# Interleave of two tensors on one core: the first store waits for the second output buffer

## The chip, the core and the metric

The kernel runs on one core of one Trainium2 chip. The time is device microseconds of one execution on that core. The kernel before has a median of 314.26 us over three runs (314.20 to 314.34).

## The reference

Two float32 tensors `x` and `y` of shape 32 x 256 x 1024 are interleaved along the last axis. Nothing is added or multiplied; every input element is copied once to its new place.

```python
result = np.zeros((batch, seq, dim * 2), dtype=np.float32)
result[..., 0::2] = x
result[..., 1::2] = y
```

Each input is 33.55 MB and the output is 67.11 MB, so at least 134.22 MB cross between HBM and SBUF.

## The kernel before, in words

**Tiles.** Each input is seen as one flat list and cut into n = 8 chunks of 128 partitions x 8192 floats (W = 8192), 4.19 MB each. A partition's row of a chunk is 32 KB and contiguous in HBM. A chunk k of `x` and a chunk k of `y` make 8.39 MB of output, which is woven and stored in two halves h = 0 and h = 1 of 4.19 MB. In what follows x2 or y2 is chunk 2 of an input, and store (1,0) is half 0 of chunk 1 of the output.

**Buffers.** There are two buffers for each input (`xt`, `yt`, chosen by the parity of k) and two output buffers (`ot`, chosen by h: half 0 always goes through `ot[0]`, half 1 through `ot[1]`).

**Loads (L45 to L55)** are issued on SyncE's queue (SP; queue q1 of the profile). Only the second half of x0 is issued on ScalarE's queue (L46). The first chunks, x0, y0, x1 and y1, are issued at the start, since there are buffers for them. From chunk 2 on, L50 makes the load of x_k wait until half 1 of chunk k-2 has had its `x` taken out of the buffer, and L54 makes the load of y_k wait for the same with `y`.

**Weaving (L57 to L70)** is done by VectorE (DVE). For every half, L67 copies 4096 columns of `xt` into the even columns of an output buffer, and L70 copies 4096 columns of `yt` into the odd ones. Each copy raises the semaphore `woven` by one, so that a half is ready at every second count: (0,0) at 2, (0,1) at 4, (1,0) at 6. Before L67 writes an output buffer again, L66 waits until the store that last read this buffer has landed.

**Stores (L72 to L78)** are issued on ScalarE's queue (ACT; queue q10 of the profile), in the order (0,0), (0,1), (1,0), (1,1) and so on. Before each one L74 waits for the `woven` count that its half needs. Each half is one DMA of 4.19 MB, except (0,0), which `parts` cuts in two: a first one of 128 x 2048 floats (1.05 MB, called piece a below) and a second one of 128 x 6144 floats (3.15 MB, piece b). ScalarE does no other work in the meantime; its queue is a list of waits and DMA issues, taken in order.

**What sets the order.** Nothing is planned by a scheduler here: the three lists (loads on SP, copies on DVE, stores on ACT) run in the written order, each held only by its semaphore waits. The two first loads are moved ahead of the opening barrier by `tile_interleave_kernel`; the change does not touch that.

**The end (L80 to L86).** ScalarE waits for all stores of half 0, SyncE for all of half 1, and the semaphores are cleared.

Of the kernel before, what the change touches and what calls it, by code (L numbers as in the profile page):

```python
# [3 lines left out]


def _interleave(nc, x, y, out):
    P = 128
    W = 8192
    H = W // 2  # L10

    total = 1
    for s in x.shape:
        total *= s
    n = total // (P * W)
    assert n * P * W == total

    def rows(ap, names, k):
        flat = ap.rearrange("b s d -> (b s d)")
        return flat[k * names : (k + 1) * names].rearrange("(p w) -> p w", p=P)  # L20

    fp32 = mybir.dt.float32
    xt = [nc.alloc_sbuf_tensor(f"xt{b}", [P, W], fp32).ap() for b in (0, 1)]
    yt = [nc.alloc_sbuf_tensor(f"yt{b}", [P, W], fp32).ap() for b in (0, 1)]
    ot = [nc.alloc_sbuf_tensor(f"ot{b}", [P, W], fp32).ap() for b in (0, 1)]

    xsem = [nc.alloc_semaphore(f"xsem{b}") for b in (0, 1)]
    hsem = nc.alloc_semaphore("hsem")
    ysem = [nc.alloc_semaphore(f"ysem{b}") for b in (0, 1)]
    woven = nc.alloc_semaphore("woven")  # L30
    osem = [nc.alloc_semaphore(f"osem{b}") for b in (0, 1)]

    xs = [rows(x, P * W, k) for k in range(n)]
    ys = [rows(y, P * W, k) for k in range(n)]
    os_ = [rows(out, 2 * P * W, k) for k in range(n)]

    Q = W // 4

    def parts(k, h):
        return [slice(0, W)] if k or h else [slice(0, Q), slice(Q, W)]  # L40

    def stored(k, h):
        return 16 * sum(len(parts(j, h)) for j in range(k))

    nc.sync.dma_start(out=xt[0][:, :H], in_=xs[0][:, :H]).then_inc(xsem[0], 16)  # L45
    nc.scalar.dma_start(out=xt[0][:, H:], in_=xs[0][:, H:]).then_inc(hsem, 16)  # L46
    for k in range(n):
        b = k % 2
        if k >= 2:
            nc.sync.wait_ge(woven, 4 * (k - 2) + 3)  # L50
        if k:
            nc.sync.dma_start(out=xt[b], in_=xs[k]).then_inc(xsem[b], 16)
        if k >= 2:
            nc.sync.wait_ge(woven, 4 * (k - 2) + 4)  # L54
        nc.sync.dma_start(out=yt[b], in_=ys[k]).then_inc(ysem[b], 16)  # L55

    for k in range(n):  # L57
        b = k % 2
        for h in (0, 1):
            c = slice(h * H, (h + 1) * H)  # L60
            if h == 0:
                nc.vector.wait_ge(xsem[b], 16 * (k // 2 + 1))
            elif k == 0:
                nc.vector.wait_ge(hsem, 16)
            if k:
                nc.vector.wait_ge(osem[h], stored(k, h))  # L66
            nc.vector.tensor_copy(out=ot[h][:, 0::2], in_=xt[b][:, c]).then_inc(woven, 1)  # L67
            if h == 0:
                nc.vector.wait_ge(ysem[b], 16 * (k // 2 + 1))
            nc.vector.tensor_copy(out=ot[h][:, 1::2], in_=yt[b][:, c]).then_inc(woven, 1)  # L70

    for k in range(n):  # L72
        for h in (0, 1):
            nc.scalar.wait_ge(woven, 4 * k + 2 * h + 2)  # L74
            for c in parts(k, h):
                nc.scalar.dma_start(
                    out=os_[k][:, h * W : (h + 1) * W][:, c], in_=ot[h][:, c]
                ).then_inc(osem[h], 16)  # L78

    nc.scalar.wait_ge(osem[0], stored(n, 0))  # L80
    used = sorted(s.num for s in [*xsem, hsem, *ysem, woven, osem[0]])
    assert used == list(range(used[0], used[-1] + 1)), used
    nc.scalar.sem_clear(range(used[0], used[-1] + 1))
    nc.sync.nop(nofuse=True).wait_op(osem[1], stored(n, 1), "sem-ge").then_inc(
        osem[1], -stored(n, 1)
    )  # L86


def kernel(tc, x, y, out):
    nc = tc.nc  # L90
    tc.close()
    tc.compile()

    _interleave(nc, x, y, out)

    blocks = nc.main_func.blocks
    for engine in (mybir.EngineType.SP, mybir.EngineType.Activation):
        opening = blocks[0].instructions
        at, moved = next(
            (b, i)  # L100
            for b in blocks[1:]
            for i in b.instructions
            if i.engine == engine and i.opcode == "DMACopy"
        )
        assert not (moved.sync_info and moved.sync_info.on_wait)
        body = at.instructions
        body.remove(moved)
        gate = next(
            n
            for n, i in enumerate(opening)  # L110
            if i.engine == engine and i.opcode == "Drain"
        )
        opening.insert(gate, moved)
        at.instructions = body
        blocks[0].instructions = opening


# [1 line left out]
_INS = ['x', 'y']  # L119
_OUTS = [((32, 256, 2048), 'float32')]  # L120


# [23 lines left out]
```

## Time and profile before

| what | value |
|---|---|
| median of three runs | 314.26 us |
| the profiled execution: its time | 314.21 us |
| the profiled execution: its span | 312.9 us |
| bytes moved | 134.22 MB (67.11 read, 67.11 written) |
| mean DMA rate over the span | 429 GB/s |
| share of 16 DMA engines: q10 (stores) and q1 (loads) | 51.3% and 48.5% |
| DVE busy | 71.9 us (23%), 32 copies of about 2.29 us |
| one 4.19 MB store, from issue to landing, median | 34.1 us |

The span goes from the first to the last instruction; the time of the execution is 1.3 us longer. The DMA shares are those of all 16 engines that move the data; both queues run on the same 16. A row of 128 partitions is split evenly, so each 4.19 MB transfer is 128 packets of 32 KB, eight on each engine. A DMA issue on a queue takes about 0.34 us of the issuing engine and says nothing of when the data moves: "to landing" does.

### The profile page before, as it was taken

The page shows a single profiled execution, that of the slowest core. Times are in us where ns is not written, and L with a number is a line of the kernel's source. Part 1 is how long each engine was busy: PE and PEld are TensorE (multiplying, and loading weights), DVE is VectorE, ACT ScalarE, POOL GpSimd, SP SyncE. Part 2 cuts the span into 40 slices and gives each one's busy share as a digit, 9 for nine tenths or more (in the row PEclk, how much of TensorE's full clock was granted, in tenths as well). Part 3 has the DMA queues.
Part 4 walks back from the last instruction along what each step waited for, and adds up shares of the span by engine and source line. Part 5 has one row for each costly group of instructions (what it writes and reads, how often), then busy time and mean ns, then how long its engine had stood idle before and what let it go on. Part 6 is the DMA issues. An engine that isn't in the chain of part 4 may idle for free.

```text
span 312.9 us, 114 instructions
## 1 busy us (share of the span) xinstructions
DVE 71.9 (23%) x32; POOL 0.2 (0%) x4
## 2 busy tenths in 40 slices
DVE  0216000501305023050230503205032050415400
POOL 0000000000000000000000000000000000000000
DMA  8999999999999999999999999999999999999998
GB/s 344 461 406 431 436 402 431 440 465 406 448 423 431 440 406 465 402 469 402 469 402 465 406 457 415 436 436 419 452 402 469 402 469 402 469 402 461 411 444 360
DMA packets 4896, 134.22 MB, mean 429 GB/s; under 512 B 544, under 2 KB 544, under 8 KB 544
## 3 DMA queue, kind: packets, MB, share of 16 engines
q10 hardware_dynamic: 2592, 69.21, 51.3%
q1 hardware_dynamic: 2304, 65.01, 48.5%
HBM read 67.11 MB, written 67.11 MB: 429 GB/s over the span
## 4 chain that ended last, share of the span: by engine, by line
DMA 82%; DVE 12%; issue 0%
DMA out_dram<-ot 76%; DMA yt<-in_y_dram 7%; DVE ot L70 6%; DVE ot L67 6%
## 5 line engine op out<-in xcount | busy, mean ns | idle before, releaser
L67 DVE COPY ot<-xt 128x4096 f32<-128x4096 f32 x16 | 36.7, 2295 | 218.0 <-DMA out_dram<-ot 206.3
L70 DVE COPY ot<-yt 128x4096 f32<-128x4096 f32 x16 | 36.6, 2288 | 8.0 <-DMA yt<-in_y_dram 8.0
L130 POOL MEMSET const-uint8-127<- 128x1 uint8 x1 | 0.1, 102 | 0.0
L130 POOL MEMSET const-bfloat16-1.0<- 128x1 bf16 x1 | 0.1, 101 | 0.0
L130 POOL MEMSET const-float32-0.0<- 128x1 f32 x1 | 0.1, 98 | 0.2 <-issue 0.2
L130 POOL MEMSET const-float32-1.0<- 128x1 f32 x1 | 0.1, 98 | 0.0
## 6 DMA issues: line engine op xcount, KB each, us to landing
out_dram<-ot ACTq DMA_DIRECT2D x15, 4096.0 KB, 34.1
yt<-in_y_dram SPq DMA_DIRECT2D x8, 4096.0 KB, 41.5
xt<-in_x_dram SPq DMA_DIRECT2D x7, 4096.0 KB, 24.4
out_dram<-ot ACTq DMA_DIRECT2D x1, 3072.0 KB, 32.8
xt<-in_x_dram SPq DMA_DIRECT2D x1, 2048.0 KB, 11.7
xt<-in_x_dram ACTq DMA_DIRECT2D x1, 2048.0 KB, 13.4
out_dram<-ot ACTq DMA_DIRECT2D x1, 1024.0 KB, 16.1
```

What stands on the lines that cost most here:

```text
L67: nc.vector.tensor_copy(out=ot[h][:, 0::2], in_=xt[b][:, c]).then_inc(woven, 1)
L70: nc.vector.tensor_copy(out=ot[h][:, 1::2], in_=yt[b][:, c]).then_inc(woven, 1)
L130: nc = _bacc.Bacc("TRN2", target_bir_lowering=False, num_devices=1)
```

## The change

The wait ahead of the first store asks for `woven` = 4 in place of 2. All other waits keep their values. The store of (0,0), in its two pieces, is therefore issued when (0,1) is woven as well, and the wait of (0,1), also 4, is then met already.

```diff
     for k in range(n):
         for h in (0, 1):
-            nc.scalar.wait_ge(woven, 4 * k + 2 * h + 2)
+            nc.scalar.wait_ge(woven, 4 * k + 2 * (h if k else 1) + 2)
             for c in parts(k, h):
                 nc.scalar.dma_start(
                     out=os_[k][:, h * W : (h + 1) * W][:, c], in_=ot[h][:, c]
                 ).then_inc(osem[h], 16)
```

No instruction is added, removed or moved on any engine; the lists of all five stand as before.

## The prediction

> **What bounds the kernel now.** I read the chain that ended last first, because it says whose work sets the end. In order of time (start us, us, what), its beginning is:
>
> ```profile
> 1.57 20.43 DMA yt<-in_y_dram
> ...
> 22.02 2.29 DVE ot L70
> 24.32 2.20 DVE ot L67
> 26.52 2.21 DVE ot L70
> ...
> 28.75 48.06 DMA out_dram<-ot
> ...
> 76.84 2.29 DVE ot L67
> 79.14 2.21 DVE ot L70
> ...
> 81.37 34.17 DMA out_dram<-ot
> ```
>
> The reader is to see that the chain runs through the weave of both halves of chunk 0, then through store (0,1), and from there alternates between a store and the 4.5 us weave behind it. Taken alone, this would say that every store sits on the path. But a store of 4.19 MB takes 34 to 48 us here, so it is not alone on the engines. Next I therefore read how fast the DMA engines move bytes, in four stretches (us, DVE, POOL, clock, DMA share, GB/s):
>
> ```profile
> 12.00:24.00 12.00, 3.98 (x2) 0.00 (x0) 1.00 1.00 431
> 24.00:46.00 22.00, 4.72 (x3) 0.00 (x0) 1.00 0.99 414
> 46.00:276.00 230.00, 53.96 (x24) 0.00 (x0) 1.00 1.00 434
> 277.00:312.00 35.00, 8.99 (x4) 0.00 (x0) 1.00 1.01 434
> ```
>
> From 12 to 24 only loads run, since no store has been issued (the first issue is at 24.35). From 46 to 276 loads and stores alternate. From 277 on only stores run: the last load is issued at 236.3, and its last packet ends at 276.2 in the trace's packet records. All three move 431 to 434 GB/s with all 16 engines busy (a window counts whole packets, so 431 and 434 are one rate). **The bound is bytes through 16 busy engines**, whichever way the bytes go: 134.22 MB / 434 GB/s = 309.3 us of the 312.9 us span. The rest is 1.0 us until the first packet, some 0.7 us of slow first packets, 0.4 us behind the last packet, and a loss in the stretch from 24 to 46, treated below.
>
> The third view is who waited for whom (total us, times, longest):
>
> ```profile
> DVE ot L67 <- DMA out_dram<-ot: 206.3, 14, 28.9
> DVE ot L67 <- DMA xt<-in_x_dram: 11.7, 1, 11.7
> DVE ot L70 <- DMA yt<-in_y_dram: 8.0, 1, 8.0
> ```
>
> DVE waits for loads only at the very start; after that, only for stores to free an output buffer. Its idle time costs nothing as long as the engines always hold some packet.
>
> **The change part by part.** *The wait.* The half (0,0) is woven at 24.31 (22.02 + 2.29), and piece a is issued at 24.35. The fourth copy ends at 28.72 (26.43 + 2.29), and store (0,1) is issued at 28.75. So pieces a and b go from 24.35 to 28.75, **4.4 us later**. Behind them on ACT stands only (0,1): it follows two issues of 0.34 to 0.46 us, so it is issued at about 29.6 in place of 28.75. That costs nothing, for it stands behind a and b in the same queue, and before the change b landed only at 57.5 (about 24.7 + 32.8). DVE's four copies and the loads of x2 (26.55) and y2 (28.75) hang on `woven` counts that this wait does not touch, and stay. SP and POOL are passed by nothing.
>
> *What runs in the 4.4 us.* x1 and y1, issued at 1.95 and 2.48, are 8.39 MB, 19.3 us at 434 GB/s, and start behind y0 at about 21. x2 and y2 join by 28.75. So the load queue has work to 40 by itself and, with x2 and y2, to about 60. The packet records show the first store packet only at 28.5, 4.1 us behind the issue; it should now be at about 32.9. Until then the engines carry loads at the 431 GB/s of the first row: **no byte of engine time is lost**, 0 us. If that cover were missing, the price would be the whole 4.4 us.
>
> *What is moved.* While both queues hold work, they share the engines packet by packet: (0,1) took from 57.5 to 76.84, 19.3 us for 4.19 MB, or 217 GB/s, half of 434. So stores run 4.4 us later, and loads 4.4 us earlier (0.95 MB at 217 GB/s each). Store (0,1) landed at 76.84; now that is at most 81.2. y2 landed at 84.15 (28.75 + 55.4, the longest landing of its line); now that is 79.8, its last packet near 78.2 (1.6 us earlier, as before). Here a stall goes in and must be priced. x3 can be issued only when the first copy of (1,1) ends, 2.3 us behind the landing of (0,1). Before, that was 79.16, 3.4 us before the load queue ran out at 82.6. Now **the load queue runs dry first**: at 78.2, with x3 issued at 82.8 to 83.5 (stores speed up a little once alone) and its first packet up to 4.1 us later. That is 5 to 9 us without loads.
>
> *Who covers that.* Store (1,0), issued near 66.5, holds 4.19 MB, 9.7 us at the 434 GB/s of the last row. It has the engines from about 79.3 to 89. Store (1,1) must be issued by then: (0,1) lands at about 80.8 (1.5 us behind its last packet), and 4.5 us of weaving give 85.3, 3.7 us ahead. So the engines stay busy, 0 us. Stores move ahead by just what loads lose; the lead that the loads had over the copies shrinks from some 34 us (y2 landed at 84.15, used at 117.86) to a few us, and the load queue should not run dry again before its end.
>
> *The end.* There the stores run alone in both kernels, and the last rows above are unchanged: (7,0) and (7,1) are issued 4.5 us behind the landing of the store two before. All bytes still pass at one rate, so what the first store lost is given back when the load queue is empty. Sum: **0 us**.
>
> *The unknown.* From 24 to 46 the profile lost (434 - 414) / 434 x 22 = 1.0 us; window edges are in that figure, and in the packet records about 0.5 us of it is real: between 27 and 32.2 the load packets of x1 took up to 1.59 us in place of 1.21, while the first stores came in. What slows them no view tells. If the first store joins after x1 is done, this can go (-0.5, at most -1.0), stay, or come a second time when x3 joins the stores (+0.5, at most +1.0). I take 0 as the middle, nearest to the row that shows it once.
>
> The sum is made against the profiled execution, 314.21 us, 0.05 below the median of 314.26: **314.2 us**.
>
> A rule speaks against the change. The Trainium skill, "DMA: Bandwidth & Descriptors", section "Rules for kernel authors", asks to issue a DMA early and wait for it late, so that its fixed cost lies beside other work; taken as a rule for time, it makes a store that is issued 4.4 us later dear, where the row of 12 to 24 says that the engines are full without it. It is the first rival.
>
> **The rivals.** *The delay stays (slower).* If the store chain simply moves, 314.2 + 4.4 = 318.6 us. It speaks for this that stores are 76% of the chain. It decides from the point where stores, once alone, would not run above the 217 GB/s that they have beside loads; the last row, 434 alone, speaks against it. Chance 0.05.
>
> *The stores run out in the dry stretch (slower).* If a store issued behind another also needs the 4.1 us that the first one needed, (1,1) would move at 89.4 against an end of (1,0) at 89: 0.4 us of idle engines. Were the stretch to return for each of the seven chunks left, that is 2.8 us, 317.0. Against it: from 277 to 312 the same handover happens twice without a dent. Chance 0.06.
>
> *The slow packets go (faster).* 313.2 to 313.7 us, as bounded above. Chance 0.10, of which 0.06 lies beyond 0.2%. *They come twice.* 314.7 to 315.2. Chance 0.05, of which 0.03 lies beyond 0.2%.
>
> *The change does not take effect* cannot be: the wait asks for 4, and (0,1) waited for the same 4 until 28.75.
>
> **How the numbers follow.** The forecast has 0.74. A measurement of this kernel can tell some 0.2%, 0.63 us, from no change. Faster: 0.06. Slower: 0.05 + 0.06 + 0.03 = 0.14. Same: the rest, 0.80. The range from 313.5 to 315.2 holds the forecast, most of the case in which slow packets go and all of that in which they come twice; the first rival and the dear end of the second stay outside.
>
> **What would show it.** In the profile after: piece a, b and (0,1) issued one behind the other from 28.75; the second chunk's first copy near 62 (57.60 before); (0,1) landed at 80 to 81.2; x3 issued at 82 to 83.5; its landing longer or shorter by the queue it meets; loads later at the end (past 276.2, near 280); windows of 434 GB/s throughout, and the last copy within 1 us of 295.7. Wrong would be: a window of 10 us behind 46 that is well below 434, an end that moves with the 4.4 us, or copies that wait for loads behind 30 us.

## The result and the profile after

The changed kernel took 317.73 us in the median of 13 executions, against 314.28 us for the kernel before in 13 executions of the same session. The ratio of the two, taken over the executions, is 1.0068, 95% interval 1.0043 to 1.0093; it is below the 1.011 of the two medians because the times of the changed kernel fall in groups. (A ratio leaves out executions over 1.5% above the fastest of their kernel: here two, 319.49 and 319.98, and in e17 below three of six, 329.38 to 334.13.) The forecast was 314.2 us, no change. What the median hides is the spread: the 13 times of the kernel before lie between 314.19 and 314.68, those of the changed kernel in groups, four at 314.4 to 314.7, one at 316.1, and the rest at 317.6 to 320.0. The kernel can run as forecast, and mostly does not.

The profiled execution took 318.31 us with a span of 317.0 us. The chain that ended last begins as the forecast said (start us, us, what):

```profile
26.46 2.21 DVE ot L70
...
28.70 0.36 ACTq L76
...
29.09 33.23 DMA out_dram<-ot
...
62.42 2.30 DVE ot L67
64.72 2.20 DVE ot L70
66.92 14.57 another core or an unknown queue
...
81.51 2.30 DVE ot L67
...
275.99 21.62 DMA out_dram<-ot
...
297.64 2.29 DVE ot L67
```

Piece a is issued at 28.70, the first copy of (1,0) starts at 62.42 (about 62 was forecast), that of (1,1) at 81.51 (80 to 81.2, so 0.3 us beyond). The piece of 14.57 us is the wait for store (0,1), for which this view finds no releaser. The last line is where the loss shows: the last weave starts at 297.64, and it was 293.51 before.

The rate of the DMA engines, in the same stretches as before with one added behind (us, DVE, POOL, clock, DMA share, GB/s):

```profile
12.00:24.00 12.00, 3.98 (x2) 0.00 (x0) 1.00 1.01 437
24.00:46.00 22.00, 4.67 (x3) 0.00 (x0) 1.00 0.99 417
46.00:276.00 230.00, 53.97 (x24) 0.00 (x0) 1.00 1.00 431
277.00:312.00 35.00, 8.99 (x4) 0.00 (x0) 1.00 1.01 433
312.00:317.00 5.00, 0.00 (x0) 0.00 (x0) 1.00 0.17 72
```

The reader is to see two things. The stretch from 24 to 46 lost no more than before (417 against 414 GB/s), and the long one fell from 434 to 431, which is 1.6 us of 230. And there is a tail: from 312 to 317 the engines are 17% busy. In a finer cut of the same view the rate falls most from 80 to 100. First the kernel before, then the changed one:

```profile
80.00:100.00 20.00, 5.02 (x3) 0.00 (x0) 1.00 0.99 428
```

```profile
80.00:100.00 20.00, 8.61 (x4) 0.00 (x0) 1.00 1.00 416
```

The share stays at 1.00 while the rate falls: the engines are not idle, their packets take longer. This is the stretch in which the load queue runs dry and joins again:

```profile
81.51 2.30 DVE L67 COPY ot<-xt 128x4096 f32<-128x4096 f32 x1 [14.60 <-DMA out_dram<-ot]
83.72 2.29 DVE L70 COPY ot<-yt 128x4096 f32<-128x4096 f32 x1
83.84 0.33 SPq L52 DMA_DIRECT2D xt<-in_x_dram  x1
86.04 0.33 SPq L55 DMA_DIRECT2D yt<-in_y_dram  x1
86.04 0.36 ACTq L76 DMA_DIRECT2D out_dram<-ot  x1
```

In the timeline from 80 to 100, x3 is issued at 83.84 and store (1,1) at 86.04. By the packet records the last load packet before ends at 79.75 and the next starts at 88.24, a dry stretch of 8.5 us (5 to 9 were forecast). Store (1,0) fills it, as forecast; no engine stands idle for more than 0.2 us. The waits are those of before as well, with no copy waiting for a load behind 30 us:

```profile
DVE ot L67 <- DMA out_dram<-ot: 210.5, 14, 33.8
DVE ot L67 <- DMA xt<-in_x_dram: 11.6, 1, 11.6
DVE ot L70 <- DMA yt<-in_y_dram: 8.0, 1, 8.0
```

So nearly every event came as forecast, and yet 4 us are lost. What no table of means shows is in the packet records. Each of the 16 engines ends its share of a transfer with a completion of its own, so the 16 completions of a transfer tell how far apart the engines are (first completion in us, and the time to the last of the 16):

```
                     before             after
y1                   46.2  +0.33        42.7  +0.75
y2                   83.4  +0.33        78.5  +2.42
store (1,0)          95.5  +0.33        91.9  +3.64
x4                  141.5  +0.33       145.6  +4.06
store (7,1), last   312.2  +0.33       312.9  +3.74
```

Before, the 16 engines stay within 0.33 us of each other from 46 us to the end. After, four of them fall behind: in the last store 12 engines are done within 0.2 us of 312.9, the other four 2.7, 2.8, 3.0 and 3.7 us later. So of the 4.1 us that the last completion comes later, 0.7 are on all engines and 3.4 are the lag of the last. The time goes to packets that take longer than the 1.21 us of a 32 KB packet, up to 2.42: behind 50 us the extra time sums to 1.20 us for each engine in the mean, 0.94 of it from 70 to 101 (0.78 from 80 to 100), against none before, and most of it falls on a few engines. The records do not name an engine, but an engine's next packet starts where its last one ended, so its packets can be strung together. Strung so, the four engines with the slow packets are four that took their first store packet at 32.2 to 32.4, one turn (one load packet) ahead of the twelve others (33.2 to 33.7): from 50 to 101 us they lost 2.4 us each in the mean, the others 0.45. **The rate of 16 engines is a mean; the end is that of the slowest one.**

The Trainium skill, "DMA: Bandwidth & Descriptors", section "Why a DMA increments its semaphore by 16 and not by 1", says that each engine posts its own increment behind its data and that only the full 16 means landed. The trace agrees: store (1,0) was complete on 12 engines at 92.2, and the copy that waited for it started at 95.89, when the last of the 16 had come at 95.5.

### The profile page after: what moved, and what is told of

The parts are those of the page before. It is cut to its first block, busy times and chain, and to the rows that moved or that the text cites. A ratio compares the mean times of both kernels' runs of the same rounds, so it can differ in the third digit from the quotient of the medians.

```text
span 317.0 us, 114 instructions
## 1 busy us (share of the span) xinstructions
DVE 72.0 (23%) x32; POOL 0.2 (0%) x4
## 4 chain that ended last, share of the span: by engine, by line
DMA 76%; DVE 13%; another core or an unknown queue 5%; issue 0%; ACTq 0%; DVEq 0%
DMA out_dram<-ot 70%; DVE ot L70 7%; DVE ot L67 6%; DMA yt<-in_y_dram 6%; ACTq L76 0%; DVEq L66 0%
## 5 line engine op out<-in xcount | busy, mean ns | idle before, releaser
L67 DVE COPY ot<-xt 128x4096 f32<-128x4096 f32 x16 | 36.7, 2295 | 222.2 <-DMA out_dram<-ot 210.5
## 6 DMA issues: line engine op xcount, KB each, us to landing
out_dram<-ot ACTq DMA_DIRECT2D x1, 3072.0 KB, 33.2
```

## The experiments

The theory after the result is **lag**: a few engines get slow packets and fall behind, and the end waits for them. Its forms differ in what starts it: R, the second joining of the loads after the dry stretch; J, the late first store as such; B, transfers of the two queues that end nearly together; P, engines that take the two queues in another order than the rest. Times are medians with the range of all executions, beside 314.2 to 314.3 for the kernel before in the same session.

**e1_after_again.** The changed kernel once more, no edit.

> The changed kernel once more, to see its spread. Theory (lag): when one DMA queue joins the other, a few of the 16 engines fall out of step and lose some us, and the end waits for the slowest of them; the time then varies by execution between about 314.4 and 320, and in the profile the 16 completions of the last store are spread by as much as the time stands above 314.4 (0.3 us spread at 314.4, 3.7 us at 318.3). Rival (delay): the 4.4 us of the first store stay in part and the spread of completions is chance; then time and spread do not go together.

Measured: 318.21 us (315.54 to 320.38, 6 executions), ratio 1.0111 (1.0084 to 1.0139). The profiled execution, 317.74 us, had its last completions at 312.7 +3.28: 13 engines on time and three late by 2.8 to 3.3 us. The three are again those that took their first store packet a turn ahead of the rest (32.2 to 32.5 against 33.2 to 33.6). Time above 314.4 and spread are near each other, 3.3 and 3.28 here, 3.9 and 3.74 in the first profile; in slower runs they are not, for e3 and e17 below end with 3.73 at 325.38 and 322.48 us. There store (6,0) has to land on the slowest engine too before (7,0) can be woven into its buffer, and the other engines wait for it (in e3 the spread is 9.57 us at 295 and 3.77 at 310).

**e2_dry_only.** The first store as before, a dry load queue by itself.

```diff
-            nc.sync.wait_ge(woven, 4 * (k - 2) + 3)
+            nc.sync.wait_ge(woven, 4 * (k - 2) + (5 if k == 3 else 3))
```

> The first store as before; only the load of x3 waits for woven 9 in place of 7, so that the load queue runs dry for some 10 to 15 us from about 82.6 on, as it did in the changed kernel for 8 us, and joins again beside running stores. Theory R (the loads' second joining makes the lag): 316 to 319 with a varying time, completions of the last store spread by 2 to 4 us. Theory J (the late first store makes the lag): 314.3, spread 0.3 us. If the stores ran out in the dry stretch, a window of 4 us there falls well below 433 GB/s.

Measured: 314.46 us (314.33 to 317.12), ratio 1.0027 (1.0009 to 1.0045). Eight of 12 executions are at 314.3 to 314.6 and four at 316.0 to 317.1. In the profile, 314.46 us, the loads were dry from 82.6 to 96.9 and came back in step: spread 0.27, later 0.14. The window from 80 to 100 stands at full rate:

```profile
80.00:100.00 20.00, 5.89 (x3) 0.00 (x0) 1.00 1.01 434
```

A dry queue costs time in a third of the executions only (no profile shows one of these, so that it is a lag there is not shown), and it does not explain 317.7. Form R is not the main cause.

**e3_late_no_dry and e4_split_control.** x3 in two halves, the first loaded as soon as its half of the buffer is free, with the late and with the early first store.

```diff
+        if k == 3:
+            nc.sync.wait_ge(woven, 4 * (k - 2) + 1)
+            nc.sync.dma_start(out=xt[b][:, :H], in_=xs[k][:, :H]).then_inc(xsem[b], 16)
         if k >= 2:
             nc.sync.wait_ge(woven, 4 * (k - 2) + 3)
-        if k:
+        if k == 3:
+            nc.sync.dma_start(out=xt[b][:, H:], in_=xs[k][:, H:]).then_inc(xsem[b], 16)
+        elif k:
...
```

The lines left out raise the count that L67's wait for `x` asks for, as x3 is now two DMAs.

> The changed kernel, but x3 is loaded in two halves, the first as soon as the first copy of (1,0) has emptied its half, about 64.7; so the load queue does not run dry near 80 and the first store is still 4.4 us late. Theory R: about 314.3, spread of the last store's completions near 0.3 to 1.5 us. Theory J: 316 to 319 and varying, as the changed kernel. Both at work: between, about 315 to 316.

> The kernel before with x3 loaded in the same two halves, nothing else: a control for the split. Both theories: 314.3 within 0.2 us. If smaller packets or a further DMA cost something of their own, it shows here and is taken off the run with the late store and the split.

Measured: late 332.05 us (319.01 to 336.63, 6 executions that differ too much for a ratio), early 314.33 us (314.26 to 315.42; ratio 1.0008, 1.0000 to 1.0017). The dry stretch is gone, and each of the six late executions is slower than each of the early ones, by 3.6 us at the least. Form R is out as the cause of that, and in this pair the dry stretch even helps: where it is missing, the lag grows from 95 us to the end of the loads, on one engine above all (9.57 us at 295). The records of the late one show where the two queues' transfers end: a store 2.4 to 2.5 us (two packets) behind a load, in every round from 120 to 260; in the early one 7.3 us ahead of it. That gave form B.

**e5_pieces4, e6_late_pieces4, e8_pieces8 and e7_dry_longer.** Four ways to move these ends against each other. In e5, e6 and e8 piece b is stored by 4, 4 and 8 DMAs of fewer partitions, each with a completion of its own in the queue; e6 has the late store and the two halves of x3 as in e3.

```diff
-        return [slice(0, W)] if k or h else [slice(0, Q), slice(Q, W)]
+        if k or h:
+            return [(slice(0, P), slice(0, W))]
+        r = P // 4
+        return [(slice(0, P), slice(0, Q))] + [
+            (slice(i * r, (i + 1) * r), slice(Q, W)) for i in range(4)
+        ]
...
```

The lines left out make the stores take these partitions too.

In e7 x3 waits longer than in e2.

```diff
-            nc.sync.wait_ge(woven, 4 * (k - 2) + 3)
+            nc.sync.wait_ge(woven, 4 * (k - 2) + (6 if k == 3 else 3))
```

> The first store as early as before; only its piece b is stored in four DMAs of 32 partitions each. On each engine a DMA is its data packets and one completion, so b has 12 packets in place of 9, and the end of a store moves 3 turns towards the end of a load, from 7 us apart to under 1 us apart. Theory B (when the two queues end a DMA within some 2 us of each other, some engines get slow packets and fall behind): clearly slower and varying, 316 to 335, with a growing spread of completions. Theory J (lateness of the first store) and theory P (an uneven joining of the engines): 314.3. Smaller packets as such: at most 1 us, 315.3.

> The late first store without a dry load queue (the run at 319 to 337), with piece b in the same four DMAs. The ends of stores and loads, which fell within 2 us of each other there, are moved 3 turns apart, some 6 to 8 us. Theory B: back to 314.3 to 314.8, spread of the last completions under 0.6 us. Theory J: 319 to 337 as without the pieces.

> The first store as before; x3 waits for woven 10 (9 in the earlier dry run), so it joins near 99.2, when by the rows of that run store (1,1), moving alone from 89.6, is ending and (2,0) begins: a load and a store then begin together, and with equal packet counts also end together from there on. Theory B: slower and varying, 316 to 335, spread growing from transfer to transfer. Theory R (each joining costs the same, wherever it falls): as the earlier dry run, 314.3 to 317.

> As the run with four pieces, but eight DMAs of 16 partitions: b has 16 packets, 7 turns more than 9, and the end of a store falls some 4 turns (10 us) behind that of a load, far from it on both sides. Theory B: 314.3 to 314.8, faster than with four pieces though it has more and smaller DMAs. If small DMAs are what costs: slower than with four pieces.

Measured: e5 314.31 us (314.22 to 315.18; ratio 1.0008, 1.0000 to 1.0017), e6 317.29 us (316.25 to 319.57; 1.0106, 1.0082 to 1.0131), e7 315.96 us (315.03 to 316.51; 1.0053, 1.0041 to 1.0065), e8 319.01 us (317.94 to 319.56; 1.0149, 1.0135 to 1.0164). Three of the four went against form B. In e5 the ends met exactly (both queues at 60.6 and at 79.9) and nothing was lost; in e6 they were over 7 us apart from 65 on and 3 us were lost all the same; e8, whose ends came out 3.6 to 6 us apart from 80 on, was the slowest. e7 decides nothing: its 315.96 us lie just under what form B expected and inside what form R did, and its spread grew only where the ends were 2.4 us apart (at 120 and 139, from 0.20 to 0.67 us) and stood still behind that. e8 has a fault as a test: a DMA of 16 partitions gave store packets of 24 KB that took up to 1.1 us longer from 41 to 65 (1.7 us for each engine in the mean), which e5 with 32 partitions had far less (at most 0.33 us, 0.06 us for each engine in the mean), so it brought a cost of its own.

**e9 to e12.** The lateness alone, in smaller steps. The two copies that weave (0,1) are cut into four each, which count on a semaphore `tick`, and the first store waits for one of them.

```diff
...
             nc.scalar.wait_ge(woven, 4 * k + 2 * h + 2)
+            if (k, h) == (0, 0):
+                nc.scalar.wait_ge(tick, 1)
```

This is e9; the wait is (tick, 2) in e10, (woven, 3) in e11 and (tick, 5) in e12. The lines left out cut the copies.

> The two copies that weave (0,1) are cut into four each, and the first store waits for the first of these pieces: it is issued some 0.6 us later than before (0.57 us of copy and what a copy costs by itself). Theory J (the later the first store, the more engines fall behind): 314.3 to 315. Theory P (what decides is where in a 1.21 us load packet the store's packets arrive, since engines near their packet's end take one load packet more than others; then some engines alternate the other way round and fall behind): half a packet from before, so the likeliest to be uneven, 315 to 319, with store piece a's completions spread by over 1 us in the profile.

> As the run before, waiting for the second piece: some 1.2 us later, one whole load packet. Theory P: as before, 314.3, spread 0.4 us. Theory J: 314.3 to 315.5, no better than the run with 0.6.

> As above, waiting for the whole first copy of (0,1), some 2.3 us later, two load packets (2.42) less a little: the first store packet is then due near 30.8, where x1 ends. Theory P: mostly as before, 314.3 to 315. Theory J: about half of what the change costs, 315.5 to 316.5.

> As above, waiting for the second piece of the second copy, some 3.4 us later, 2.8 load packets. Theory P: uneven in some executions, 314.3 to 318. Theory J: three quarters of the change, 316.5 to 317.5.

Measured (issue of the first store in the profile, its lateness against 24.35, time, ratio):

```
     issue   late   median (all)                ratio
e9   25.25   0.9    314.52 (314.24 to 315.52)   1.0011 (1.0001 to 1.0021)
e10  25.75   1.4    315.05 (314.43 to 316.43)   1.0026 (1.0013 to 1.0039)
e11  26.86   2.5    319.90 (318.90 to 320.95)   1.0178 (1.0154 to 1.0202)
e12  28.00   3.7    316.86 (315.91 to 316.99)   1.0074 (1.0058 to 1.0089)
```

Later is not always worse: 2.5 us late costs more than 3.7 or the change's 4.4. So J does not hold as a price for each us. What form P said of the four beforehand failed as well: e9, uneven as expected (completions of piece a 2.16 us apart), lost only 0.3 us, e10 was to be as before and is 0.8 us slower, and e11, to be mostly as before, is the slowest. But e11 does not speak against P itself: 15 engines took their first store packet at 31.1 to 31.5 and one at 32.9, and that one lost 3.4 us to slow packets from 50 to 101, the others 0.5 in the mean, and ended the last store 3.76 us behind the rest.

**e13 to e16.** Is an uneven order of the two queues needed, and is it enough? In e13 and e14 all stores stand on SP's queue between the loads, so there is one order only, with the late and the early first store (and the clearing of the semaphores at the end moved to ScalarE alone). In e15 and e16 an extra load of 4 or 16 rows of 64 floats, into an unused tile, stands ahead of the first store.

```diff
...
+    load(0)
+    load(1)
+    for k in range(n):
+        for h in (0, 1):
+            nc.sync.wait_ge(woven, 4 * k + 2 * (h if k else 1) + 2)
+            for c in parts(k, h):
+                nc.sync.dma_start(
+                    out=os_[k][:, h * W : (h + 1) * W][:, c], in_=ot[h][:, c]
+                ).then_inc(osem[h], 16)
+        if k + 2 < n:
+            load(k + 2)
...
```

This is e13. In e14 the wait is `4 * k + 2 * h + 2`, as before; the stores on ACT's queue are gone in both. Then e15; in e16 both 4s are 16. The lines left out make the tile and its semaphore and wait for the load at the end.

```diff
...
+            if (k, h) == (0, 0):
+                nc.scalar.dma_start(out=tt[:4], in_=xs[0][:4, :64]).then_inc(tsem, 16)
...
```

> All stores are issued on SP's queue, between the loads in a written order (store (k,0), store (k,1), x of k+2, y of k+2), so that every engine has one list and no queue joins another; the first store waits for woven 4. Theory P (engines that take the two queues in another order than the rest fall behind): 314.3 to 314.7, spread of the last completions under 0.6 us, in every execution. Theory J (lateness as such): 316 to 319. If the alternation of reads and writes packet by packet is of use in itself, both one-queue kernels are slower alike.

> The same with one queue, the first store waiting for woven 2 as before: the control. Both theories: as the late one under theory P, 314.3 to 314.7, since the store stands behind y1 in the queue until about 41 either way.

> The kernel before, with one extra load of 4 x 64 floats into an unused tile on ACT's queue just ahead of the first store. It moves 1 KB and has packets on 4 of the 16 engines only, so those 4 take the first store packet one or two load packets later than the other 12. Theory P: 315.5 to 319, varying, spread of the last completions 1.5 to 4 us, though the first store is not late. Theory J: 314.3.

> The same extra load with 16 x 64 floats: a packet on each of the 16 engines, so all are shifted alike. The control for the run with 4. Theory P: mostly 314.3 to 314.8, well below the run with 4. If any small DMA at this place does harm: as the run with 4.

Measured: e13 317.49 us (317.12 to 317.96; ratio 1.0104, 1.0091 to 1.0117), e14 318.01 us (317.30 to 318.63; 1.0119, 1.0104 to 1.0134), e15 314.77 us (314.35 to 315.43; 1.0019, 1.0011 to 1.0028), e16 314.61 us (314.12 to 316.48; 1.0016, 1.0003 to 1.0028). An uneven order is neither needed for a lag nor enough for a large one. With one list for all engines a lag grows too, step by step from 0.53 us at 61 to 2.56 us at 235 in e13, late or early alike. And the order made uneven costs 0.5 us in e15, whose engines ended within 0.59 us of each other although seven of them had taken their first store packet a turn or two behind the rest; e16, with all 16 shifted alike, is 314.61 and so no better clear of noise. Form P as the only cause falls; that the engines out of step are the ones that fall behind in the changed kernel, e1 and e11 stands. The windows of e14 show that this, too, is a lag and no idle queue, since share and rate stay up until the last slices:

```profile
100.00:276.00 176.00, 40.48 (x18) 0.00 (x0) 1.00 1.00 431
277.00:312.00 35.00, 8.99 (x4) 0.00 (x0) 1.00 1.00 433
```

**e17_late_whole and e18_early_whole.** (0,0) is stored by one DMA, so that all packets beside running loads have 32 KB, with the late and with the early first store.

```diff
-        return [slice(0, W)] if k or h else [slice(0, Q), slice(Q, W)]
+        return [slice(0, W)]
```

> The changed kernel with (0,0) stored by one DMA of 32 KB packets, so that no piece a gives way to a piece b and stores and loads have packets of one size from the start. Theory T (the passage from the small to the larger pieces beside running loads is what puts engines out of step when it comes late): 314.2 to 314.8 in nearly every execution, last completions spread under 0.6 us. If any late first store does it: 316 to 320 as the changed kernel.

> The kernel before with (0,0) stored by one DMA: the control. Theory T: 314.2. If the pieces are what keeps the kernel before in step, this one is slower, 315 to 319, and the early store has nothing to do with it.

Measured: late 325.93 us (three executions at 320.37 to 322.48 and three at 329.38 to 334.13; ratio 1.0223, 1.0188 to 1.0259), early 314.52 us (314.29 to 315.01; 1.0006, 0.9998 to 1.0015). The passage between pieces is not needed. But the pair is the plainest of all: one number in one wait, and some 7 us by the ratios (11 by the medians of all executions). The windows of the late one, profiled at 322.48 us:

```profile
46.00:150.00 104.00, 22.48 (x10) 0.00 (x0) 1.00 1.01 427
150.00:280.00 130.00, 31.47 (x14) 0.00 (x0) 1.00 1.00 423
280.00:312.00 32.00, 8.99 (x4) 0.00 (x0) 1.00 0.98 423
312.00:321.00 9.00, 0.00 (x0) 0.00 (x0) 1.00 0.62 266
```

and of the early one:

```profile
46.00:150.00 104.00, 27.26 (x12) 0.00 (x0) 1.00 1.00 432
150.00:280.00 130.00, 27.26 (x12) 0.00 (x0) 1.00 1.01 436
280.00:312.00 32.00, 8.99 (x4) 0.00 (x0) 1.00 0.99 426
```

The late one loses all the way (427, then 423 GB/s) at a DMA share of 1.00, and its completions drift from 0.5 us apart at 50 to 5.7 us at 285. The early one keeps 0.42 to 0.45 us to the end. In the late one all engines joined in step (first store packets at 33.9 to 34.4), its loads never ran dry between 46 and 280, and no data packet beside the stores is small. What differs is where a store's end falls against a load's: 2.4 to 3.2 us behind it in the late one, 7.3 us ahead of it in the early one, in every round, since both have the same number of packets.

## Why the prediction was wrong

**What bounds the kernel** held as a mean and failed as a bound. The rows of 431 to 434 GB/s were taken to say that time is bytes over a rate. They are sums over 16 engines, and in the kernel before sum and slowest engine agree, because all 16 completions stay within 0.33 us. The prediction never asked whether they do, and no term of its sum could hold an engine that falls behind. Two of its own signs did show that something was wrong: the last copy started at 299.85, not within 1 us of 295.7, and the profiled end moved by 4.1 us.

**The wait, 4.4 us later:** right (28.70, and 62.42 for the first copy of chunk 1). **What runs in the 4.4 us, 0 us:** right; the 24 to 46 stretch moved 417 GB/s against 414. What it did not show is that four engines took their first store packet at 32.2 to 32.4 and twelve at 33.2 to 33.7, one load packet later, so that the completions of piece a lay 1.36 us apart (0.40 before). These four are the ones that then fell behind.

**The dry stretch and who covers it:** its place, its length (8.5 us) and its cover by store (1,0) were right. Store (1,1) was issued at 86.04 (85.3 forecast) and no engine stood idle for more than 0.2 us. The step failed in its last clause, "So the engines stay busy, 0 us": they stay busy with slower packets. The stretch from 80 to 100 holds the larger part of the extra packet time (0.78 of 1.20 us for each engine; 416 against 428 GB/s). But e3 and e17, which have no dry stretch there and lose more, show that it is a place where the lag grows, and not its source.

**The unknown** is the term of the sum that was mis-sized. The slow packets of the first joining were put at 0.5 us as a mean over engines, at most 1.0, and allowed to come a second time. The first joining cost the same as before, 0.51 us for each engine (0.52), and the second time measured 1.20 us in the mean, a little beyond the bound; what decided was that it fell on three or four engines, which ended 2.7 to 3.7 us behind the rest. A bound on the mean was used as a bound on the slowest.

**The rivals:** none names what happened. The delay did not stay: four executions of 13 took 314.4 to 314.7 with the same late issue in the program, and 12 of the 16 engines ended only 0.7 us later in the profiled one. That its 318.6 lies near the profiled 318.31 is chance; e17 loses 6 to 20 us to a store 4.4 us late. The stores did not run out in the dry stretch. "They come twice" is the nearest, with 314.7 to 315.2 and a chance of 0.05.

**What starts the lag is only partly settled.** Shown by pairs that differ in one wait: with the same work, a late first store costs 3.5 us in the change, 11.4 us in e17 against e18, and some 18 us in e3 against e4, all by the medians of all executions; in the last two pairs every late execution is slower than every early one. Shown not to be needed or not to suffice: the dry queue (e3, e17), lateness in proportion (e11 against e12), an uneven first order (e13, e15, and e3 and e17, whose engines joined in step), the small pieces (e17). Which engines fall behind in the changed kernel, e1 and e11 goes with that first order; why their packets are the slow ones is not shown. Open, then: why packets become slow. There is an association, formed after the runs and not tested by one of its own: the two kernels whose loads and stores end 1.5 to 3.2 us apart in every round from 44 to 270 us (e3, e17) are the two slowest, and their lag grows to the end of the loads; those where they stay 5.5 to 7.3 us apart (before, e4, e18) lose nothing; those that are within 2.5 us in some rounds and 4.8 us or more apart in the others (the changed kernel, e6, e7, e11, e12) lie between, at 316 to 320. e5, with ends exactly together until 80, and e16, with 2.4 us until 81 and 314.6 us, do not fit it, e8 has its own cost, and one queue (e13, e14) lies outside it. The late store changes this distance, from 7.3 us to 1.2 to 2.0 us before the dry stretch and 4.8 us behind it; that this is how it acts is argued and not shown.

No version tried beats the kernel before.

## What to carry to other kernels

When all DMA engines are busy, a change in the order of transfers need not be free: here it cost 0.7% in the change and 2.2% in e17, by the ratios. The rate is a mean over 16 engines, and a transfer lands, and a kernel ends, with the slowest; so look at how far apart the 16 completions of a transfer lie, and at the tail of the last slices, before calling such a change neutral. A kernel whose times agree within 0.2% may owe that to an order that happens to keep the engines in step; time a reordering over many executions, since one good one (314.43 here) proves nothing.

## What the runs showed of the hardware

- A 32 KB packet takes 1.21 us nearly always, alone or with the other queue taking turns. Now and then packets on a few engines take up to 2.42 us in the changed kernel and up to 3.59 in e3, with all engines busy, and the engines then stay apart to the end.
- A transfer is eight data packets and one completion on each engine, and the completion takes a turn of its own between two queues: in the kernel before, two load packets pass on each engine between the last data packet of a store and the first of the next (2.09 us from the last engine's end at 75.30 to the first engine's start at 77.39).
- The first packet of a DMA on an empty queue comes some 4 us behind its issue when the other queue is busy (24.35 to 28.49 before, 83.84 to 88.24 after), and 1.0 us when the engines are idle.
- One queue for loads and stores was slower than two (318.01 against 314.2), though both keep the engines full.
